# Two-layer hybrid trunk on one core: narrow products merged, padded and ordered by array tile, and constants made at the start

## Chip, cores and metric

One core of one Trainium2 chip runs the whole program. The metric is the device time of one execution in microseconds (us), the median of several runs. Engines are named as the profile names them: PE is TensorE's matmuls, PEld its weight loads, DVE VectorE, ACT ScalarE, POOL GpSimd, and SP the engine from whose queue all data transfers are issued.

## The reference

The input is 256 tokens of width 1024. Each of the two layers projects the normalized input `h` into the columns of three token mixers, runs the mixers, merges them under gates, and then runs a feed-forward part: dense in the first layer, eight experts (two per token) in the second. Cut to what the change touches:

```python
def layer(x, l):
    h = rms_norm(x) * (1 + sc_m) + sh_m
    rw_cols, ssd_cols, fox_cols, gates = split(h @ w_in[l])
    # 1. RWKV-7: token shift, low-rank decay / rate / gate, delta-rule recurrence
    r, k, v, w_lo, a_lo, g_lo = split(token_shift(rw_cols, mu))   # 512 512 512 64 64 160
    w = -softplus(-(w0 + tanh(w_lo) @ w_up)) - 0.5
    a = sigmoid(a0 + a_lo @ a_up);  g = sigmoid(g_lo) @ g_up
    if l > 0: v = v + (v_first - v) * sigmoid(v0 + (h @ v_down) @ v_up)   # v_down: 1024x32
    S_t = S_{t-1} * w_t + (S_{t-1} a_t) b_t + v_t k_t ;  y_t = S_t r_t     # per head, 64x64
    # 2. SSD: 16 heads in 4 groups, dt = softplus(dt_raw + bias), chunks of 128 tokens
    a_cum = cumsum(dt * A);  decay_ij = exp(a_cum_i - a_cum_j)             # per head, 128x128
    # 3. FoX: 8 heads of 64, softmax attention with a cumulative log-forget bias
    s = q @ k.T / 8 + F_q - F_k,  F = cumsum(log_sigmoid(f_logit + bias))
    x = x + g_m * (merged @ w_out[l]);  x = x + g_f * ffn(...)
```

## The kernel before

Activations stand with features on the 128 partitions and the 256 tokens along the free axis. Every weight arrives in float32 and is split into a high part (ACT, L156) and a low part (DVE, L157); a product of such pairs is three one-pass matmuls (`mm3`). The small matrices inside the mixers are plain float32, and the trace shows each of their products as two passes, that is two MATMUL records. Transposes (`transpose`, L131) are one pass.

A planner that simulates the engines writes each engine's order when the program is built; on the chip each engine then runs its queue in that order. `ORDER` names the steps of a layer: `r0`, `r1` are the two halves of RWKV (two 128-feature blocks each), `s0` to `s3` the SSD groups, `f0`, `f1` the halves of FoX, `G`, `m0` to `m2` gates and merges. Steps of different mixers alternate, so that the projections of one run between the dependent steps of another.

The projections use two PSUM buffers named `pd` (`dbank`), taken in turn; the mixers use four named `pm` (`mbank`) and two named `ps` (`sbank`). Places that the change touches:

- `small_cols` projects 24 columns (16 `dt`, 8 forget logits), copies them and transposes them into `dtr` (L452, L454, L456). `rwkv` then projects 288 columns from 1536 (L470), as a block of 256 and one of 32 (the last 32 of the gate LoRA), and in the second layer 32 more (`rw_v_down`, L479).
- `rwkv_half`, first stage: 16 products of 64 rows each per half (L611), head by head, copied out by DVE (L612). Second stage: a triangular inverse in six levels; each level ends in DVE transposes (L654). Its end is L682 to L691. Third stage: the recurrence over two chunks (L693 to L731). Fourth: `gu0` and `gu1` (L751, L752), the latter with 32 rows.
- `ssd` makes the cumulative sums of 16 heads (L781 to L784), high and low part; `ssd_group` copies one head's row to all partitions by two products with 16 rows (L838).
- `fox_half` transposes 64 features of q and k per head (L927, L928), and makes the bias row for partition 64 by three products with one column (L929 to L931).
- Masks and identities are built in the first layer after the first normalization (L1320 to L1372); six products (L1365) and their DVE work build `ztmask`.

## Time and profile before

| | |
|---|---|
| median of 3 runs | 2226.83 us (2225.98 to 2227.79) |
| profiled execution | 2224.52 us, of which span 2222.8 us |
| PE busy (share of the span) | 2115.0 us (95%) |
| DVE busy | 1798.8 us (81%) |
| ACT busy | 1386.1 us (62%) |
| POOL busy | 152.1 us (7%) |
| data moved | 546.68 MB, mean 246 GB/s |

The first layer's mixers stand at about 45 to 450 us, its output projection and feed-forward part at 450 to 705, the second layer's mixers at 705 to 1150, and the experts from there to the end. A PE record's duration holds the latency of the array; how fast a run of n matmuls streams is read from the starts of successive rows, or from a merged row as (length of the run minus one duration) over n-1.

### The profile page before, as it was taken

Reading aid. Unit: us, or ns where it says so; the run is one execution under the profiler, and the core shown is the slowest. Engines: PE = TensorE matmul, PEld = TensorE weight load, DVE = VectorE, ACT = ScalarE, POOL = GpSimd, SP = SyncE. Lnnn points to the kernel's source line nnn. Section 1 sums busy time; section 2 is a strip of 40 time slices with the busy share of each in tenths; the row PEclk is TensorE's granted clock in tenths of the full one; section 3 lists DMA queues with packets and bytes.
Section 4 is the critical chain, followed back from the end, with each engine's and each line's share of the span. In section 5 each row is a group of like instructions: output and inputs, shape, how many; then the busy total and the mean of one; then the engine's idle time right before and its main releaser. Section 6 shows DMA issues by size and latency. Waiting matters only on the chain.

```text
span 2222.8 us, 35724 instructions
## 1 busy us (share of the span) xinstructions
PE 2115.0 (95%) x13489; PEld 1811.2 (81%) x13489; DVE 1798.8 (81%) x2822; ACT 1386.1 (62%) x2204; POOL 152.1 (7%) x180
## 2 busy tenths in 40 slices
PE   7899899999998889989998999999999999999998
PEld 4777789998997877868998788888888887888776
DVE  4977776777776797756768999999999989999887
ACT  3454455555454545434555877878878777878775
POOL 2211200000000031211002000000000000000000
PEclk9999999999999998988998999999999999999999
DMA  8423254667884533414556999999999999999994
GB/s 304 128 83 95 77 172 156 213 198 259 294 286 137 145 108 93 138 53 130 184 176 251 337 362 359 324 368 367 374 337 352 355 362 336 342 364 368 336 363 151
DMA packets 316101, 546.68 MB, mean 246 GB/s; under 512 B 11952, under 2 KB 143536, under 8 KB 315920
## 3 DMA queue, kind: packets, MB, share of 16 engines
q1 hardware_dynamic: 315920, 544.31, 71.1%
q8 instruction: 108, 1.77, 0.3%
q14 instruction: 73, 0.60, 0.1%
HBM read 543.22 MB, written 1.05 MB: 245 GB/s over the span
## 4 chain that ended last, share of the span: by engine, by line
PE 79%; DVE 13%; issue 3%; ACT 2%; DMA 2%; POOL 0%; SPq 0%; DVEq 0%; ACTq 0%; POOLq 0%
PE pd L122 37%; PE pm L122 33%; PE ps L122 7%; DVE lo L157 5%; PE pm L131 1%; DVE u L654 1%; DMA araw<-in_ada_w_dram 1%; PE ps L131 1%; ACT hi L156 1%; DMA b<-in_ada_w_dram 1%; DVE cu L802 1%; DVE xr L1257 1%; DVE u L225 0%; DMA raw<-in_moe_w_gu_dram 0%; DVE b L612 0%
## 5 line engine op out<-in xcount | busy, mean ns | idle before, releaser
L156 ACT ACTIVATE hi<-raw 128x1024 fp32r<-128x1024 f32 (+2 forms) x1201 | 1027.7, 870 | 522.4 <-PE pd L122 277.0
L157 DVE TENSOR_TENSOR lo<-raw,hi 128x1024 fp32r<-128x1024 f32 (+2 forms) x1197 | 1154.6, 990 | 211.6 <-ACT hi L156 189.8
L122 PE MATMUL pd<-hh,hi 128*128 128x256 f32 (+2 forms) x1208 | 352.7, 293 | 15.3 <-ACT hh L362 3.9
L122 PE MATMUL pd<-hh,lo 128*128 128x256 f32 (+2 forms) x1208 | 346.5, 287 | 0.0
L122 PE MATMUL pd<-hl,hi 128*128 128x256 f32 (+2 forms) x1208 | 345.7, 286 | 0.3
L122 PE MATMUL pm<-lo,hh 128*128 128x512 f32 x672 | 266.7, 397 | 3.0 <-DVE lo L157 2.8
L122 PE MATMUL pm<-hi,hh 128*128 128x512 f32 x672 | 266.9, 397 | 0.1
L122 PE MATMUL pm<-hi,hl 128*128 128x512 f32 x672 | 263.0, 392 | 0.0
L122 PEld LDWEIGHTS pd<-hh,hi 128*128 128x128 f32 (+2 forms) x1208 | 231.9, 192 | 28.3 <-issue 5.6
L122 PEld LDWEIGHTS pd<-hh,lo 128*128 128x128 f32 (+2 forms) x1208 | 231.5, 192 | 6.1 <-issue 3.9
L122 PEld LDWEIGHTS pd<-hl,hi 128*128 128x128 f32 (+2 forms) x1208 | 232.7, 193 | 4.3 <-issue 2.3
L122 PE MATMUL pd<-lo,hi 128*128 128x512 f32 x448 | 174.7, 390 | 0.0
L122 PE MATMUL pd<-hi,hi 128*128 128x512 f32 x448 | 170.9, 391 | 0.1
L122 PE MATMUL pd<-hi,lo 128*128 128x512 f32 x448 | 167.8, 389 | 0.0
L122 PEld LDWEIGHTS pm<-lo,hh 128*128 128x128 f32 x672 | 126.8, 189 | 32.1 <-DVE lo L157 5.5
L122 PEld LDWEIGHTS pm<-hi,hh 128*128 128x128 f32 x672 | 126.5, 188 | 29.3 <-ACT hi L156 1.4
L122 PEld LDWEIGHTS pm<-hi,hl 128*128 128x128 f32 x672 | 126.7, 189 | 26.5
L122 PE MATMUL pm<-hi,more 128*128 128x512 f32 x448 | 142.1, 392 | 0.0
L122 PEld LDWEIGHTS pd<-hi,hi 128*128 128x128 f32 x448 | 84.1, 188 | 18.4 <-ACT hi L405 0.5
L122 PEld LDWEIGHTS pd<-hi,lo 128*128 128x128 f32 x448 | 84.1, 188 | 17.8
L122 PEld LDWEIGHTS pd<-lo,hi 128*128 128x128 f32 x448 | 84.1, 188 | 17.6
L122 PEld LDWEIGHTS pm<-hi,more 128*128 128x128 f32 x448 | 84.1, 188 | 17.5 <-ACT hi L156 0.3
(423 smaller groups left out, 3467.0 us busy)
## 6 DMA issues: line engine op xcount, KB each, us to landing
raw<-in_moe_w_gu_dram SPq DMA_DIRECT2D x224, 1024.0 KB, 7.0
raw<-in_moe_w_down_dram SPq DMA_DIRECT2D x110, 1024.0 KB, 6.8
raw<-in_w_in_dram SPq DMA_DIRECT2D x66, 1024.0 KB, 5.4
araw<-in_ada_w_dram SPq DMA_DIRECT2D x68, 512.0 KB, 4.3
raw<-in_ffn_w_gu_dram SPq DMA_DIRECT2D x22, 1024.0 KB, 6.8
raw<-in_ffn_w_down_dram SPq DMA_DIRECT2D x11, 1024.0 KB, 6.5
raw<-in_w_in_dram SPq DMA_DIRECT2D x16, 512.0 KB, 5.1
raw<-in_proj_ssd_dram SPq DMA_DIRECT2D x8, 1024.0 KB, 5.2
```

The lines of the kernel that those rows point to most:

```text
L122: pe.matmul(o, lhsT, rhs, start=start, stop=stop)
L131: pe.transpose(o, i, ident[:n, :n])
L156: act.activation(hi, raw, AF.Copy)
L157: minus.tensor_sub(lo, raw, hi.bitcast(F32))
L654: dve.transpose(blk(bds[ch], q)[:, odd, bcol(q)], by4(blk(pz, q))[:, odd, :])
L802: dve.scalar_tensor_tensor(cu[:, s:T], ps[:, 0:T - s], pph[:, w:w + 1], cu[:, s:T], op0=ALU.mult, op1=ALU.add)
L1257: dve.tensor_add(xr[:, t, hs], xr[:, t, hs], po)
```

## The change

`small_cols` now makes one projection of 88 columns: the 32 of the gate LoRA, 32 of `rw_v_down` (zeros in the first layer), 16 `dt`, 8 forget logits. It leaves them in `gl[:, 1, :]`, whose other partitions are zero, and transposes that tile whole. The products with `gu1` and `vup` take all 128 rows, with zeros in the padding. `cum` holds the high part on partitions 0 to 15 and the low part on 32 to 47, so that one product with 128 rows does for two with 16. In FoX the cumulative sums are made once per layer and written as a 65th feature beside k (ones beside q), and the transposes carry it. Products in the first and third stage of RWKV and at the end of the second are regrouped by the rows and columns of the array that they use. The constants (`identb`, `uincl`, `ustr`, `mmask`, `nmq`, `headsel`, `bones`, `rmask`, `icomp`, `ztmask`), by the same lines as before, move from behind the first normalization to the place between the first loads and the first products.

```diff
@@ setup
-    identr = const("identr", [16, 16], F32R)
-    act.activation(identr, ident[:16, :16], AF.Copy)
+    identr = const("identr", [P, 16], F32R)
+    dve.tensor_tensor(identr, ident[:, 0:16], ident[:, 32:48], op=ALU.add)
@@ load_lora
-        gu1 = keep("gu1", [32, RW])
-        nc.sync.dma_start(gu1, lora_g[l])
+        gu1 = keep("gu1", [P, RW])
+        pool.memset(gu1, 0.0)
+        nc.sync.dma_start(gu1[0:32], lora_g[l])
@@ accumulate
-        step = min(kin, stage[2] // w)
+        step = min(kin, 1 << (stage[2] // w).bit_length() - 1)
@@ small_cols
-        raw = load_raw(dtw[l].rearrange("p (k w) -> p k w", k=KD), KD, 24)
+        gl = mx("gl", [P, 2, T], bufs=1 + (l > 0))
+        pool.memset(gl[:, 1, :], 0.0)
+        raw = load_raw(narrow[l].rearrange("p (k w) -> p k w", k=KD), KD, 88)
         ps = dbank()
-        accumulate(ps[:24, :T], raw, (hh, hl))
-        dc = mx("t1", [24, T], bufs=2)
-        act.activation(dc, ps[:24, :T], AF.Copy)
+        accumulate(ps[:88, :T], raw, (hh, hl))
+        act.activation(gl[64:88, 1, :], ps[64:88, :T], AF.Copy)
+        if l > 0:
+            act.activation(gl[32:64, 1, :], ps[32:64, :T], AF.Copy)
+        shift(prm, gl[:32, 1, :], ps[:32, :T], 14)
+        ps = dbank().rearrange("p (a t) -> p a t", t=P)
         for t in range(2):
-            transpose(ps[:, T + t * 24:T + t * 24 + 24], dc[:, t * P:(t + 1) * P], 24)
+            transpose(ps[:, t, :], gl[:, 1, t * P:(t + 1) * P])
@@ rwkv
-        project_cols(w_in[l], 1536, 288, lambda i, ps: shift(wa if i == 0 else gl[:ps.shape[0], i - 1, :], ps, 12 + i))
+        project_cols(w_in[l], 1536, 256, lambda i, ps: shift(prm, wa if i == 0 else gl[:, 0, :], ps, 12 + i))
...
-            accumulate(ps[:32, :T], load_raw(rw_v_down.rearrange("p (k w) -> p k w", k=KD), KD, 32), (hh, hl))
-            vd = mx("wa", [32, T], bufs=2)
-            act.activation(vd, ps[:32, :T], AF.Copy)
-            vup = mx("gl", [32, RW], bufs=2)
-            nc.sync.dma_start(vup, rw_v_up)
+            vup = mx("gl", [P, RW], bufs=2)
+            pool.memset(vup, 0.0)
+            nc.sync.dma_start(vup[32:64], rw_v_up)
@@ rwkv_half, first stage
+                pss = [mbank(), mbank()]
+                for jj in J:
+                    for hb in range(2):
+                        hp = hblock(hb)
+                        mm(pss[hb][:, jj * 256:jj * 256 + 256], src[hp, jj, cs], ar[jj][hp, ch, :, :])
                 for hb in range(2):
-                    ps = mbank()
-                    hp = hblock(hb)
-                    for jj in J:
-                        mm(ps[:, jj * 256:jj * 256 + 256], src[hp, jj, cs], ar[jj][hp, ch, :, :])
                     dve.copy_predicated(dst.rearrange("p (j b) m t -> p j b (m t)", b=2)[:, :, hb],
                                         mmask.rearrange("p m t -> p (m t)").unsqueeze(1).broadcast_to([P, 2, 2 * P]),
-                                        ps.rearrange("p (q m) -> p q m", q=2))
+                                        pss[hb].rearrange("p (q m) -> p q m", q=2))
@@ rwkv_half, end of the second stage
+        yas = []
         for ch in range(2):
             py = mbank()[:, :256].rearrange("p (q t) -> p q t", q=4)
...
-            ya = unit(mx, 4, 64)
-            act.activation(ya[h1], py[h1], AF.Copy)
+            yas.append(unit(mx, 4, 64))
+            act.activation(yas[ch][h1], py[h1], AF.Copy)
+        for ch in range(2):
+            ya = yas[ch]
@@ rwkv_half, third stage
             for q, (jj, hp, f) in enumerate(heads):
-                o = pb[q % 2][:, jj, :]
-                mm(o, mk[:, q, 0, :], vrow[:, ch, f], True, ch == 0)
-                if ch == 1:
-                    mm(o, ar[jj][hp, 1, 0, :], s0[hp, jj, :], False, True)
+                mm(pb[q % 2][:, jj, :], mk[:, q, 0, :], vrow[:, ch, f], jj == 0, ch == 0 and jj == 1)
+            if ch == 1:
+                for q, (jj, hp, f) in enumerate(heads):
+                    mm(pb[q % 2][:, jj, :], ar[jj][hp, 1, 0, :], s0[hp, jj, :], False, jj == 1)
...
+            py = mbank()[:, :256].rearrange("p (j t) -> p j t", j=2)
+            for q, (jj, hp, f) in enumerate(heads):
+                mm(py[hp, jj, :], vrow[:, ch, f], mk[:, q, 1, :], jj == 0, False)
+            if ch == 1:
+                for q, (jj, hp, f) in enumerate(heads):
+                    mm(py[hp, jj, :], s0[hp, jj, :], ar[jj][hp, 1, 1, :], False, False)
...
             if ch == 0:
                 pst = mbank().rearrange("p (q f) -> p q f", f=64)
...
                 dve.tensor_tensor(s0, pst[:, 0:2, :], dec0.unsqueeze(2).broadcast_to([P, 2, 64]), op=ALU.mult)
+            for q, (jj, hp, f) in enumerate(heads):
+                mm(py[hp, jj, :], sa[:, q, :], mb[:, q, 1, :], False, jj == 1)
+            yc = unit(mx, 2, P)
+            act.activation(yc, py, AF.Copy)
@@ rwkv_half, fourth stage
-            mm(pg[:, jj * T:(jj + 1) * T], gu1[:, js], gl[0:32, 1, :], False, True)
+            mm(pg[:, jj * T:(jj + 1) * T], gu1[:, js], gl[:, 1, :], False, True)
@@ ssd and ssd_group
-            mm(ps[:16, ch * P:(ch + 1) * P], dta[:, ch * 16:ch * 16 + 16], uincl)
+            mm(ps[:48, ch * P:(ch + 1) * P], dta[:, ch * 16:ch * 16 + 48], uincl)
+        cum = mx("cum", [P, T], F32R)
+        pool.memset(cum.bitcast(F32), 0.0)
...
-                for i in range(2):
-                    mm(pc[:, e * T:(e + 1) * T], identr[:, h:h + 1].broadcast_to([16, P]), cum[:, i, :], i == 0, i == 1)
+                mm(pc[:, e * T:(e + 1) * T], identr[:, h:h + 1].broadcast_to([P, P]), cum)
@@ fox and fox_half
+        ps = mbank()
+        mm(ps[:, 0:8], uincl, nlf[:, 0:8])
+        mm(ps[:, 8:16], uincl, nlf[:, 8:16], True, False)
+        mm(ps[:, 8:16], ones, nlf[:, 0:8], False, True)
+        sums = small(16, "f", 10).rearrange("p (t h) -> p t h", t=2)
+        act.activation(sums, ps[:, 0:16].rearrange("p (t h) -> p t h", t=2), AF.Copy)
...
-            o = unit(mx, 2, 256)
+            o = mx("u", [P, 2, 4, 65 if g < 2 else 64], bufs=NUNIT)
...
+            if g == 0:
+                pool.memset(o[:, :, :, 64:65], 1.0)
+            elif g == 1:
+                pool.tensor_copy(o[:, :, :, 64], sums[:, :, 4 * hf:4 * hf + 4])
...
-                    transpose(ps[0:64, t * P:(t + 1) * P], qkv[1][:, t, f])
-                    transpose(ps[0:64, T + t * P:T + (t + 1) * P], qkv[0][:, t, f])
-                mm(ps[64:65, 0:P], nlf[:, h:h + 1], uincl)
-                mm(ps[64:65, P:2 * P], nlf[:, 8 + h:9 + h], uincl, True, False)
-                mm(ps[64:65, P:2 * P], nlf[:, h:h + 1], ones, False, True)
+                    transpose(ps[0:65, t * P:(t + 1) * P], qkv[1][:, t, h, :])
+                    transpose(ps[0:65, T + t * P:T + (t + 1) * P], qkv[0][:, t, h, :])
@@ main
     first_load(6)
     first_load(7)
+
+    identb = const("identb", [P, P], BF16)
+    dve.tensor_copy(identb, ident)
...
+        ztmask.append(ztm)
+        prev = same
+
     first_half(0)
...
-            done = norm_cols(mod_affine(l, 1, 0, prm["pp"][:, NMIX:NMIX + 8]), normed)
+            norm_cols(mod_affine(l, 1, 0, prm["pp"][:, NMIX:NMIX + 8]), normed)
             dump(f"hh{l}", hh)
-            if l == 0:
-                with tc.issue_after(done.ins):
-
-                    identb = const("identb", [P, P], BF16)
...
-            dtr = small_cols(l, mx)
+            dtr, gl = small_cols(l, mx, prm)
```

## Rows read from the trace of the kernel before

**Rows 1.** The page: the chain that ended last, by engine, as shares of the span.

```profile
PE 79%; DVE 13%; issue 3%; ACT 2%; DMA 2%; POOL 0%; SPq 0%; DVEq 0%; ACTq 0%; POOLq 0%
```

**Rows 2.** Busy time by stage: stretch, its length, then busy us (and instructions) of PE, PEld, DVE, ACT, POOL, the granted share of PE's clock, the DMA share and GB/s.

```profile
45.00:300.00 255.00, 229.83 (x1963) 195.45 (x1962) 197.00 (x480) 121.37 (x287) 52.30 (x59) 0.94 0.35 104
...
705.00:1050.00 345.00, 308.86 (x2502) 262.60 (x2503) 250.96 (x571) 167.95 (x394) 62.19 (x66) 0.91 0.38 114
1050.00:1150.00 100.00, 100.00 (x843) 94.08 (x841) 68.18 (x128) 55.79 (x120) 3.95 (x3) 1.00 0.53 168
```

**Rows 3.** The chain that ended last, by line, in the stretches 60 to 300 us (first row), 300 to 450 (second) and 735 to 1050 (third).

```profile
by line: PE pd L122 34.1%; PE pm L122 18.0%; PE ps L122 8.7%; DVE lo L157 5.7%; DVE u L654 5.3%; PE pm L131 3.4%; issue 3.2%; DVE cu L802 2.7%; ACT s L843 1.9%; ACT hi L156 1.9%; DVE b L612 1.2%; DVE u L225 0.8%; DVE s L848 0.8%; PE ps L131
by line: PE pd L122 71.2%; PE pm L122 14.3%; PE ps L122 8.9%; PE pm L131 4.2%; ACT hi L156 0.8%; PE ps L131 0.4%; ACT u L953 0.3%; issue 0.1%; ACTq L156 0.0%
by line: PE pd L122 41.5%; PE pm L122 19.0%; PE ps L122 8.4%; DVE u L654 4.5%; issue 3.7%; PE pm L131 3.7%; DVE lo L157 2.6%; DVE u L225 2.1%; DVE cu L802 1.9%; DVE b L612 1.4%; DVE u L223 1.2%; ACT hi L156 0.8%; DVE s L822 0.5%; DVE xb L80
```

**Rows 4.** PE's waits, 45 to 450 us (first row) and 705 to 1150 us (second): what waited for what, us in total, times, longest us.

```profile
PE pm L122 <- DVE u L654: 8.4, 9, 1.7
PE pm L122 <- DVE u L654: 8.5, 9, 2.4
```

**Rows 5.** PE in order of time around 305 us, in FoX: start us, length of the run us, instruction, count.

```profile
304.91 0.60 PE L131 MATMUL pm<-ident,u 128*64 128x128 f32 x4
305.44 0.60 PE L122 MATMUL pm<-uincl,sm 128*1 128x128 f32 x4
...
306.19 0.52 PE L131 MATMUL pm<-ident,u 128*64 128x128 f32 x3
```

**Rows 6.** The same around 319 us, in an SSD group.

```profile
319.14 0.28 PE L122 MATMUL pd<-hl,hi 128*128 128x256 f32 x1
319.25 0.39 PE L122 MATMUL pd<-hh,lo 128*128 128x256 f32 x2
319.57 0.73 PE L122 MATMUL ps<-cum,identr 16*128 16x256 f32 x4
320.23 0.39 PE L122 MATMUL pd<-hh,hi 128*128 128x256 f32 x1
```

**Rows 7.** The same around 85 us (a 256-column float32 product with all rows), around 265 us (fourth stage of RWKV) and 734 us (`vup`).

```profile
85.35 0.59 PE L122 MATMUL pm<-u,bones 128*128 128x256 f32 x2
85.78 0.27 PE L131 MATMUL pm<-ident,vfirst 128*128 128x128 f32 x1
...
265.83 0.70 PE L122 MATMUL pm<-gl,up 128*128 128x256 f32 x2
...
268.34 0.44 PE L131 MATMUL pm<-ident,u 128*128 128x128 f32 x2
...
734.38 0.69 PE L122 MATMUL pm<-wa,gl 32*128 32x256 f32 x2
735.00 0.39 PE L122 MATMUL pd<-hh,lo 128*128 128x256 f32 x1
```

**Rows 8.** The same around 165 and 176 us, in the third stage of RWKV.

```profile
165.41 0.44 PE L122 MATMUL pm<-s,u 64*128 64x64 f32 x4
...
166.87 0.43 PE L122 MATMUL pm<-s,u 64*128 64x64 f32 x2
...
176.36 0.44 PE L122 MATMUL pm<-u,s 64*64 64x128 f32 x4
```

**Rows 9.** The products of L611, around 90 and 780 us.

```profile
90.09 2.10 PE L122 MATMUL pm<-u,u 64*128 64x256 f32 x16
...
780.33 1.13 PE L122 MATMUL pm<-u,u 64*128 64x256 f32 x4
781.39 0.39 PE L122 MATMUL pd<-hl,hi 128*128 128x256 f32 x1
```

**Rows 10.** Mask work at 40 to 62 us, grouped by line: count, busy us, mean ns.

```profile
L1365 PE MATMUL pm<-u 32*128 32x128 f32 (+4 forms) x10 | 2.1, 308 | 0.0
L1366 DVE COPY u<-pm 128x128 f32<-128x128 f32 x6 | 1.7, 286 | 0.4 <-PE pm L1365 0.4
L1370 DVE TENSOR_TENSOR ztm<-u,ustr 128x128 bf16<-128x128 f32 x6 | 1.7, 285 | 0.0
```

**Rows 11.** The projections of 32 columns on PE at 0 to 1160 us, one of their three parts (the other two have as many): count, busy us, mean ns, idle before.

```profile
L122 PE MATMUL pd<-hh,hi 128*32 128x256 f32 x24 | 6.7, 280 | 1.0 <-ACT dtr L456 1.0
```

**Rows 12.** PE and DVE in order of time at the start of the second layer's mixers.

```profile
713.75 0.41 PE L122 MATMUL pd<-hh,lo 128*24 128x256 f32 x1
713.96 0.41 PE L122 MATMUL pd<-hh,hi 128*24 128x256 f32 x1
...
719.31 0.48 DVE L363 SCALAR_TENSOR_TENSOR hl<-h,mod,hh 128x256 fp32r<-128x256 f32 x1
...
720.86 0.28 PE L122 MATMUL pd<-hh,lo 128*128 128x256 f32 x1
...
722.53 0.30 PE L122 MATMUL pd<-hh,hi 128*32 128x256 f32 x1 [0.67 <-ACT dtr L456]
...
730.88 0.28 PE L122 MATMUL pd<-hh,hi 128*128 128x256 f32 x1
```

**Rows 13.** SP's queue and POOL in order of time in the first 20 us.

```profile
15.50 0.63 SPq L286 DMA_DIRECT2D gu<-in_lora_g_dram  x1
...
17.53 3.55 POOL L605 MEMSET b<- 128x2048 f32 x2 [14.06 <-PE ps L122]
```

More of the change, by code (lines that the diff above doesn't have):

```diff
@@ L65, in trunk @@
     ctx: ExitStack, tc: tile.TileContext,
-    x, cols, heads, dtw, ada_w, w_in, lora_up, lora_g, rw_v_down, rw_v_up, proj_rw, proj_ssd, proj_fox, w_out,
+    x, cols, heads, narrow, ada_w, w_in, lora_up, lora_g, rw_v_up, proj_rw, proj_ssd, proj_fox, w_out,
     ffn_w_gu, ffn_w_down, moe_router, moe_w_gu, moe_w_down, out, dbg=None, stop=None,
@@ L1297, in trunk @@
     first_load(7)
+    identb = const("identb", [P, P], BF16)
+    dve.tensor_copy(identb, ident)
+    uincl = const("uincl", [P, P])
+    pool.affine_select(out=uincl, in_=ones, compare_op=ALU.is_ge, fill=0.0, base=0,
+                       pattern=[[1, P]], channel_multiplier=-1)
+    ustr = const("ustr", [P, P])
+    pool.affine_select(out=ustr, in_=ones, compare_op=ALU.is_gt, fill=0.0, base=0,
+                       pattern=[[1, P]], channel_multiplier=-1)
+    mmask = const("mmask", [P, 2, P], U8)
+    dve.tensor_copy(mmask[:, 0, :], ustr)
+    dve.tensor_copy(mmask[:, 1, :], uincl)
+    nmq = const("nmq", [P, P], BF16)
+    dve.tensor_scalar(nmq, ustr, -1e30, None, op0=ALU.mult)
+    headsel = const("headsel", [P, 2])
+    pool.memset(headsel, 0.0)
+    pool.memset(headsel[0:64, 0:1], 1.0)
+    pool.memset(headsel[64:128, 1:2], 1.0)
+    bones = const("bones", [P, P])
+    pool.memset(bones, 0.0)
+    pool.memset(bones[0:64, 0:64], 1.0)
+    pool.memset(bones[64:128, 64:128], 1.0)
+    rmask = const("rmask", [P, 4, P], BF16)
+    pool.memset(rmask, 1.0)
+    pool.memset(rmask[:, :, 0:1], 0.0)
+    icomp = const("icomp", [P, P])
+    for n in range(4):
+        ns = slice(n * 32, n * 32 + 32)
+        dve.tensor_copy(icomp[ns].rearrange("p (q c) -> p q c", q=4), ident[ns, ns].unsqueeze(1).broadcast_to([32, 4, 32]))
+    ztmask = []
+    prev = ident
+    for lv in range(6):
+        m2 = 2 << lv
+        nb = P // m2
+        same = unit(mx, 1, P)[:, 0, :]
+        ind = unit(mx, 1, P)[:, 0, :]
+        pool.affine_select(out=ind[:nb], in_=ones[:nb], compare_op=ALU.is_ge, fill=0.0, base=0,
+                           pattern=[[1, P]], channel_multiplier=-m2)
+        pool.affine_select(out=ind[:nb], in_=ind[:nb], compare_op=ALU.is_ge, fill=0.0, base=m2 - 1,
+                           pattern=[[-1, P]], channel_multiplier=m2)
+        ps = mbank()
+        pe.matmul(ps[:, :P], ind[:nb], ind[:nb], start=True, stop=True)
+        dve.tensor_copy(same, ps[:, :P])
+        ztm = const(f"ztm{lv}", [P, P], BF16)
+        diff = unit(mx, 1, P)[:, 0, :]
+        dve.tensor_sub(diff, same, prev)
+        dve.tensor_mul(ztm, diff, ustr)
+        ztmask.append(ztm)
+        prev = same
     first_half(0)
```

138 lines of the change are left out of this document (38 added, 100 removed).

## The prediction

> **What bounds the kernel.** I read the chain that ended last first: PE holds 79% of it and DVE 13% [rows 1]. Then the stages. The change leaves the feed-forward parts alone; it acts in the two layers' mixers. There the reader is to separate two kinds of stretch. In the second part of each layer's mixers (FoX, the last SSD group, the merges) PE is the chain: the second row of rows 3 adds up to 99%, and in the second layer PE is busy for all of the 100 us [rows 2, 3]. In the first part PE's lines add up to about 65% of the chain in the first layer and 73% in the second; the rest is mostly DVE steps of the RWKV recurrence [rows 3], and PE is busy in 230 of 255 and 309 of 345 us [rows 2]. So a microsecond of PE work taken out is worth a full one in the second part, and in the first part about what PE's share of the chain says, 0.69 on average. That share is my exchange rate; the true one lies between 0 and 1.
>
> The price of PE's work is read from starts of successive rows, not from durations. A one-pass 256-column product costs 0.11 us [rows 6]. A change between array shapes costs extra: the product before the run of 16-row products keeps 0.20 instead of 0.11 us for its last pass (0.32 from 319.25 to 319.57 for two), and the run of four takes 0.66 where four of the usual kind would take 0.45 [rows 6].
>
> **The change, part by part.**
>
> FoX. From the first transpose to the next head's first, 304.91 to 306.19, a head takes 1.28 us; six of its ten passes are the one-column sums. Four transposes at 0.11 (the four passes at 305.44 hold 0.43) leave 0.44, so 0.84 goes per head [rows 5]. That the 65th column makes a transpose dearer no row shows; its pass still streams 128 columns of the identity, so I take nothing. 16 heads in two layers: 13.4 us. Added are six passes a layer before the halves, at 0.11: 1.3. Net 12.1, in the second part, at full rate. POOL's writes of the 65th feature are ready long before the transposes.
>
> Cumulative sums of SSD. Each pair of heads spends 0.66 plus 0.09 of the shape change; two full-height passes cost 0.23 [rows 6]. 0.52 times 16 pairs is 8.3 us. A quarter (the last group of each layer) lies in the second part at full rate, 2.1; 6.2 lie in the first part.
>
> Padding. The fourth stage's eight passes take 2.51 us, 265.83 to 268.34; at 0.215 a pass (two in 0.43, 85.35 to 85.78) they would take 1.72 [rows 7]: 0.78 in four halves, 3.1 us. `vup` takes 0.62 instead of 0.43, plus 0.09 on entry [rows 7]: 0.28 four times, 1.1 us.
>
> Recurrence. In the second chunk full-height and half-height products alternate: five runs that start 0.37 apart, 1.8 us in all [rows 8]. Grouped, I estimate 1.25 (four full passes at 0.11, eight half-height passes at the pace of the first run of rows 8, and two changes of shape). 0.55 four times is 2.2; two changes fewer in `py` and two fewer at the second stage's end give 1.2 and 0.7 at 0.09 each over all halves and chunks. Sum 4.1 us. The `s0` products of `py` work with both row halves in one PSUM bank; in the trace four such passes run in 0.44 us [rows 8], less than one after the other. The Trainium skill (TensorEngine Tiling (Array Packing), Gotcha 1) says that different row tiles cannot use one bank at a time; the trace does not bear that out here, and by the rule some 0.6 us of this term would be lost.
>
> These first-part terms (6.2, 3.1, 1.1, 4.1) make 14.5 us of PE time; at 0.69, 10.0.
>
> The products of L611. Where the planner already lets two row halves run side by side, 16 passes take about 1.8 us; where it does not, four take 1.06 [rows 9]. The new order makes pairs everywhere: four lone sets in each half, two groups of two each saving 0.3, some 2.4 us a half and 9.6 in all at most. But these sets wait for DVE's copies (L612 is itself in the chain [rows 3]), and two buffers are now taken at once. Between 0 and 9.6 I take 2.0, nearest the end at which DVE decides.
>
> Constants. Ten passes of L1365, 2.1 us, stand between the first projections, and about 0.4 of shape changes with them; at the start PE waits for loads, so they cost nothing there. DVE's part is 1.7 (L1366), 1.7 (L1370) and about as much for the rest [rows 10], 6.8 us in all, moved to where DVE waits for the first loads. Of it only the entries after about 57 us, where DVE becomes the chain, count: 1.2. Sum 3.7; ends 2.5 and 9.3. If the cover at the start were gone, the six products would delay the first normalization by at most their own 2.1 us.
>
> Narrow projections. 72 one-pass products go (24 rows of each of three parts [rows 11]); at 0.115 that is 8.3 us, 2.75 in the first layer and 5.5 in the second. It doesn't come in full. Before, PE fills the time in which the normalization delivers its eight column blocks with two groups, the 24-column one and the first 128 of the 256; in the second layer that ends at 720.86, while the last block is delivered at about 719.8 [rows 12]. After, the narrow product takes one `pd` buffer and the transposes take the other, so the 256-wide block has to wait until the narrow one has been copied out: two or three copies of ACT and one DVE step, some 1.5 us. Second layer: last block 719.8, copies to 721.4, 48 products at 0.114 to 726.9, where before the six groups end at 730.88 [rows 12]. That is 4.0 at the full clock, and -0.7 if all 48 run at the 0.21 us spacing of 713.75 to 713.96 [rows 12]; I take 2.4, a third of them slow. First layer, by the same reckoning with one group less to save, 1.1. Sum 3.5, ends -2.7 and 8.2.
>
> Waits that are added. `gu1` and `vup` are now cleared by POOL before SP may issue their loads, and behind those in SP's queue stand the first projection weights. The load of `gu1` is issued at 15.50; POOL's next work, clears that wait for PE, starts at 17.53 [rows 13]. If the planner puts the new clear ahead of those it costs nothing, which I take; behind them it could hold SP for several microseconds, the upper end of the range.
>
> **Sum.** 12.1 + 2.1 + 10.0 + 2.0 + 3.7 + 3.5 = 33.4 us. Against the profiled execution, 2224.52 us (span 2222.8, with 1.7 around it, 2.3 below the median of the runs), 2191.1; against the median, 2226.8 - 33.4 = 2193.4. The experts start earlier by as much, and their stage is not touched.
>
> **Rivals.**
>
> Waits take PE's place: in the first part every PE saving turns into waiting for DVE. For it: DVE is busy in 197 of 255 us there [rows 2]. Against it: PE's named waits are short, 8.4 us for the longest group in the first layer [rows 4]. Then 10.0 and 2.0 go: 2205.4. With the narrow term at its lower end and SP held as well, it is 2219, inside the bound of no change with a little more.
>
> The clock stays low at the mixers' start. Products are 0.21 us apart at 713 and 0.11 at 720 [rows 12], the 1.2 and the 2.4 GHz level; PE was full between. With only one narrow group, PE pauses between blocks. Then the narrow term is -2.7: 2199.6. The Trainium skill (TensorE: Matmul & The Clock Gate, HAM oscillation) says the clock is throttled by default and released by sustained activity, which speaks against thinning this stretch; the spacing agrees.
>
> The regrouping does not reach the chip, since the planner sorts by its own forecast (it already interleaves row halves that the source has in series [rows 9]): recurrence and L611 give nothing, 2.8 + 2.0: 2198.2.
>
> Better: exchange rate 1, L611, constants and narrow products at their upper ends: 12.1 + 2.1 + 14.5 + 9.6 + 9.3 + 8.2 = 55.8, 2171.
>
> Slower: the work removed was what filled the waits of the triangular inverse. 40 of its steps end in DVE's transposes (five levels, two chunks, four halves), and only 18 of them now make PE wait, 16.9 us in all, 0.42 per step [rows 4]. If every step waited the longest of the first layer, 1.7, it would be 68 us, 51 more, and the time 2244. It decides from (16.9 + 33.4)/40 = 1.26 us a step. Against it: the projections, the main filler, stay.
>
> **Chances.** Forecast 0.46; waits 0.16; low clock 0.10; no regrouping 0.12; better 0.06; slower 0.05; the stacked case near no change 0.05. The range, 2174 to 2212, leaves out most of "better", all of "slower" and the stacked case. About 0.2% (4.5 us) is what a measurement of this kernel can tell from no change: faster 0.89, same 0.06, slower 0.05.
>
> **What would show it.** Right: no one-column sums in FoX and 0.44 us per head; two passes per pair of SSD heads with no stretched pass before them; eight even passes in RWKV's fourth stage; no L1365 after 10 us; the first layer's mixers shorter by about 18 us and the second's by about 15.5. Wrong: PE's waits for L654, L612 or L648 growing by more than 10 us; products at 0.21 spacing well after the normalization ends; SP idle before 20 us; DVE's share of the chain in the first part rising by as much as PE's falls.

## The result, and the profile after

The changed kernel takes 2199.12 us (median of 4 runs, 2196.64 to 2200.93) where the kernel before takes 2227.31 on the same chip: a ratio of 0.9871, 95% interval 0.9854 to 0.9888, or 29 us less (25 to 33). A second set of five rounds gave 0.9875 (0.9852 to 0.9899). The forecast was 2193.4 with a range from 2174 to 2212, faster. The profiled execution took 2199.16 us, span 2197.1.

The first two fences answer to [rows 1] and [rows 2]. First the page's chain by engine, then busy time by stage (columns as in [rows 2]).

```profile
PE 78%; DVE 14%; issue 3%; DMA 3%; ACT 3%; POOL 0%; SPq 0%; DVEq 0%; ACTq 0%; POOLq 0%
```

```profile
45.00:300.00 255.00, 230.89 (x1921) 196.82 (x1922) 192.25 (x454) 120.97 (x288) 50.73 (x59) 0.89 0.35 102
705.00:1050.00 345.00, 310.15 (x2608) 274.00 (x2609) 261.52 (x597) 178.10 (x415) 59.19 (x66) 0.92 0.39 116
1050.00:1150.00 100.00, 98.58 (x826) 94.99 (x826) 70.79 (x129) 56.20 (x115) 2.33 (x1) 1.00 0.55 177
```

PE still holds the chain. (The granted clock is a share of 2.4 GHz; 0.50 is the level of 1.2.) In the first layer PE is as busy over the 255 us as before, though it has less to do: its granted clock in that stretch is 0.89, before 0.94. (In the second profile of the changed kernel, further down, it is 0.93.)

Most operations came out as forecast. Each group of the next fence is PE in order of time: FoX's transposes, a pair of SSD heads, the fourth stage of RWKV, the recurrence, the first stage's products, and the last products of the masks (start us, length of the run us, instruction, count; the first five answer to [rows 5 to 9]).

```profile
308.26 1.03 PE L132 MATMUL pm<-ident,u 128*65 128x128 f32 x8
309.13 0.27 PE L132 MATMUL ps<-ident,xb 128*128 128x128 f32 x1
...
321.25 0.28 PE L123 MATMUL pd<-hl,hi 128*128 128x256 f32 x1
321.37 0.40 PE L123 MATMUL ps<-cum,identr 128*128 128x256 f32 x2
321.61 0.28 PE L123 MATMUL pd<-hh,lo 128*128 128x256 f32 x1
...
299.95 0.60 PE L123 MATMUL pm<-gl,up 128*128 128x256 f32 x2
...
301.68 0.27 PE L132 MATMUL pm<-ident,u 128*128 128x128 f32 x1
...
292.11 0.66 PE L123 MATMUL pm<-s,u 64*128 64x64 f32 x8
292.70 0.66 PE L123 MATMUL pm<-b,u 128*64 128x128 f32 x8
293.29 0.65 PE L123 MATMUL pm<-u,s 64*64 64x128 f32 x8
293.87 0.39 PE L123 MATMUL pd<-hh,hi 128*128 128x256 f32 x1
...
218.07 1.13 PE L123 MATMUL pm<-u,u 64*128 64x256 f32 x8
...
222.79 1.13 PE L123 MATMUL pm<-u,u 64*128 64x256 f32 x4
...
19.33 0.79 PE L1357 MATMUL pm<-u 2*128 2x128 f32 x2 [1.82 <-POOL u L1354]
```

Eight transposes with the 65th column take 0.87 us, so a head takes 0.44, and the column costs nothing. A pair of SSD heads takes 0.24 (321.37 to 321.61) where it took 0.66, and no pass ahead of it is stretched. The fourth stage's eight passes take 1.73 us where [rows 7] have 2.51. The recurrence's eight passes with `s` stand in one run, 0.59 us to the next row, instead of three ([rows 8]). The eight `s0` products of `py` (293.29 to 293.87) take 0.58 us, as long as the eight full-height passes ahead of them, so the 0.6 us that the prediction set against them were not lost. Two things did not come. L611's regrouping (L615 after) hardly reached the chip: 13 lone sets of four passes remain, as many as before, and a lone set (222.79) is as long as eight passes whose row halves run side by side (218.07). And the masks' products, which were to be over by 10 us, wait for POOL; the last pair runs at 19.33.

What did not come as forecast are the stages. I read each stage from the starts of the same seven steps in every trace. In the changed kernel they are: the first `s + 1` of RWKV's first half, the scaling of the second half's first chunk, the first addition of the output projection, the end of the feed-forward part (the second of the two steps of that row), the same `s + 1` and scaling in the second layer, and its last merge.

```profile
66.35 0.43 DVE L520 TENSOR_SCALAR u<-u 128x512 f32<-128x512 f32 x1 [0.37 <-ACT u L519]
295.56 0.42 DVE L752 TENSOR_TENSOR u<-u,sm 128x256 f32<-128x256 f32 x1 [1.12 <-POOL sm L135]
479.69 0.41 DVE L1022 TENSOR_TENSOR xr<-xr,h 128x256 f32<-128x256 f32 x1
698.22 1.29 DVE L1069 TENSOR_TENSOR xr<-xr,otmp 128x512 f32<-128x512 f32 x2
742.78 0.42 DVE L520 TENSOR_SCALAR u<-u 128x512 f32<-128x512 f32 x1
985.00 0.42 DVE L752 TENSOR_TENSOR u<-u,sm 128x256 f32<-128x256 f32 x1 [1.19 <-POOL sm L135]
1147.68 0.41 DVE L1011 TENSOR_TENSOR b<-b,gt 128x256 f32<-128x256 f32 x1
```

The differences of these starts, for the profiled execution of each kernel in this study (us; "start", "first part" and "second part" of each layer's mixers, and between the layers the output projection with the feed-forward part):

| kernel | start 1 | first 1 | second 1 | between | start 2 | first 2 | second 2 | span |
|---|---|---|---|---|---|---|---|---|
| before | 61.2 | 227.0 | 196.6 | 220.3 | 45.8 | 246.8 | 173.3 | 2222.8 |
| before, second profile | 62.5 | 228.1 | 196.6 | 221.1 | 45.3 | 246.3 | 173.5 | 2225.1 |
| changed | 66.4 | 229.2 | 184.1 | 219.1 | 44.0 | 242.2 | 162.7 | 2197.1 |
| changed, second profile | 67.6 | 223.4 | 183.9 | 221.8 | 44.3 | 242.8 | 162.0 | 2196.1 |
| sums alone | 63.7 | 230.7 | 194.8 | 223.2 | 45.6 | 249.1 | 173.2 | 2230.8 |
| sums and FoX | 64.4 | 224.8 | 186.5 | 222.8 | 46.1 | 252.1 | 167.7 | 2213.9 |
| padding of `gu1` alone | 63.3 | 230.6 | 193.7 | 220.2 | 45.7 | 249.8 | 172.7 | 2228.2 |
| regrouping alone | 62.1 | 228.8 | 194.8 | 220.2 | 45.9 | 239.7 | 167.2 | 2212.6 |
| regrouping undone | 66.3 | 234.2 | 187.3 | 220.1 | 44.7 | 253.0 | 166.3 | 2226.5 |
| narrow products undone | 64.3 | 224.0 | 185.1 | 220.2 | 45.7 | 243.0 | 163.7 | 2200.5 |
| constants undone | 67.7 | 221.8 | 184.4 | 221.4 | 43.8 | 242.4 | 161.9 | 2197.9 |
| narrow product later | 60.6 | 222.3 | 184.3 | 220.4 | 43.9 | 238.5 | 161.3 | 2183.7 |
| narrow product in `ps` | 59.9 | 222.7 | 185.6 | 221.7 | 37.7 | 248.0 | 159.9 | 2189.7 |
| both of these | 64.5 | 223.6 | 184.0 | 225.3 | 39.7 | 246.1 | 162.4 | 2198.4 |

In the profiled pair the second parts give 12.5 and 10.6 us, 23 of the 26 that the span fell by. The first layer's start loses 5.2; the first parts give -2.2 and 4.6. So the gain sits in the second parts, and hardly at all in the first ones. These second parts are not quite the stretches where the prediction counted PE's work at full rate: they begin at 295.6 and 985.0 and hold the last steps of the recurrence, and in the second layer the regrouping alone takes 6.2 of the 10.6 us there.

A row of the table is one execution. Those of the sums alone and of the padding alone are the slowest of their kernels' runs, 3.5 and 4.4 us above the median; that of the narrow product in `ps` is 5.7 above it.

The start of the first layer shows its loss in the trace. The next fence has ACT and PE in order of time; the last row is the pause of PE that the narrow term named.

```profile
32.24 0.89 ACT L157 ACTIVATE hi<-raw 128x352 fp32r<-128x352 f32 x2 [1.65 <-DMA raw<-in_narrow_dram]
33.03 0.36 ACT L354 ACTIVATE u<-ps 128x256 f32<-128x256 f32 x1
...
46.48 0.66 PE L132 MATMUL pd<-ident,gl 128*128 128x128 f32 x2 [2.03 <-DVE gl L452]
```

ACT's queue has the split of the narrow weights ahead of the copy that the normalization waits for, and those weights land at 32.2; before, that copy ran at 28.05. (The experiments show that this is not what sets the pace.) Then the narrow product holds one `pd` buffer and its transposes the other, and PE waits for the copies. The second layer's start shows the same (PE in order of time, answers to [rows 12]):

```profile
718.26 0.66 PE L132 MATMUL pd<-ident,gl 128*128 128x128 f32 x2 [2.39 <-DVE gl L452]
718.57 0.56 PE L123 MATMUL pd<-hh,hi 128*128 128x256 f32 x1
...
722.77 0.35 PE L123 MATMUL pd<-hl,hi 128*128 128x256 f32 x1
722.96 0.29 PE L123 MATMUL pd<-hh,lo 128*128 128x256 f32 x1
723.08 0.28 PE L123 MATMUL pd<-hh,hi 128*128 128x256 f32 x1
```

The last block of the normalized input is ready at 714.6 + 0.5 us; the 256-wide block starts at 718.57 and runs at 0.21 us a product until 722.8, then at 0.11.

### The profile page after: what moved, and what is told of

Same layout as the page of the kernel before. It is cut to its first block, busy times and chain, and to the rows that moved or that the text cites. A ratio compares the mean times of both kernels' runs of the same rounds, so it can differ in the third digit from the quotient of the medians.

```text
span 2197.1 us, 35356 instructions
## 1 busy us (share of the span) xinstructions
PE 2092.7 (95%) x13301; PEld 1804.3 (82%) x13301; DVE 1798.8 (82%) x2822; ACT 1380.2 (63%) x2204; POOL 151.7 (7%) x187
## 4 chain that ended last, share of the span: by engine, by line
PE 78%; DVE 14%; issue 3%; DMA 3%; ACT 3%; POOL 0%; SPq 0%; DVEq 0%; ACTq 0%; POOLq 0%
PE pd L123 37%; PE pm L123 31%; PE ps L123 7%; DVE lo L158 6%; PE pm L132 1%; DVE u L658 1%; ACT hi L157 1%; PE ps L132 1%; DVE cu L811 1%; DMA b<-in_ada_w_dram 1%; DMA araw<-in_ada_w_dram 1%; DMA raw<-in_narrow_dram 1%; DVE xr L1270 0%; DMA raw<-in_moe_w_gu_dram 0%; DMA raw<-in_proj_ssd_dram 0%
## 5 line engine op out<-in xcount | busy, mean ns | idle before, releaser
L123 PE MATMUL pd<-hh,hi 128*128 128x256 f32 (+1 forms) x1184 | 349.4, 295 | 9.9 <-DVE cu L811 3.3
L123 PE MATMUL pd<-hl,hi 128*128 128x256 f32 (+1 forms) x1184 | 341.7, 289 | 1.8 <-DVE hl L365 1.8
L123 PE MATMUL pd<-hh,lo 128*128 128x256 f32 (+1 forms) x1184 | 340.4, 288 | 0.2 <-DVE lo L158 0.2
L123 PEld LDWEIGHTS pd<-hh,hi 128*128 128x128 f32 (+1 forms) x1184 | 231.2, 195 | 26.3 <-issue 10.2
L123 PEld LDWEIGHTS pd<-hl,hi 128*128 128x128 f32 (+1 forms) x1184 | 231.6, 196 | 8.4 <-DVE hl L365 4.6
L123 PEld LDWEIGHTS pd<-hh,lo 128*128 128x128 f32 (+1 forms) x1184 | 230.8, 195 | 3.3 <-issue 2.4
L123 PEld LDWEIGHTS pd<-hi,lo 128*128 128x128 f32 x448 | 84.0, 188 | 17.8 <-DVE lo L408 0.2
```

The lines of the kernel that those rows point to most:

```text
L123: pe.matmul(o, lhsT, rhs, start=start, stop=stop)
```

## Experiments

Each kernel was timed against the kernel before on its chip; ratios are to that, with 95% intervals.

**Which part delays the start?** Four kernels were made from the changed one. The first has its narrow products and their padding as before (each line with its old counterpart put back: `dtw`, `rw_v_down`, `project_cols(..., 1536, 288, ...)`, `gu1` and `vup` of 32 rows).

> The changed kernel (2199.1 us) with its narrow products as before: 24 columns, then 256 and 32, then 32 of v_down, and gu1 and vup with 32 rows; everything else stays changed. In the changed kernel the tanh of the decay input comes 7.8 us later in the first layer (54 for 46 us) and, measured from the start of the layer, 7 us later in the second. Theory A, the merged narrow product starves the start of the mixers (its transposes hold the second pd buffer, PE pauses and the 256-wide block runs at 0.21 us a product): without it the tanh is back at 46 to 48, the second layer's start is 7 us shorter, and of these 15 us most shows in the time, less 2.9 for the padding that also goes: 2186 to 2194. Rival B, the late start is absorbed by waits that are there anyway: the narrow term of the prediction (3.5) and 2.9 of padding come back, 2205. Rival C, the constants at the start made it late: the tanh stays at about 54, 2203 to 2206. Theory D, apart from these: between 89 and 117 us the changed kernel runs PE at the low clock, 0.21 instead of 0.11 us a product, for some 13 us; where that stretch is at the high clock in this run, the time falls by up to 13 more.

Measured: 2203.15 us, ratio 0.9892 (0.9876 to 0.9909), some 4 us slower than the changed kernel, with intervals that overlap. The tanh comes at 49.5 us (54 in the changed kernel, 46 before) and the second layer's start takes 17.8 us to it, as before (26.7 in the changed kernel). Theory A is right on where a part of the time goes at the start (64.3 instead of 66.4 and 67.6 us, where 61.2 and 62.5 stood before), and wrong on its weight: 26.7 or 17.8 us to the tanh, `s + 1` comes 44.0 or 45.7 us into the second layer. That wait is absorbed by the next one, as rival B said. With the padding gone as well, 2205 was B's number. Theory D fails too: the first layer's first part runs at 0.94 of the clock here, and the time did not fall.

The second has the constants behind the normalization, as before:

```diff
-            norm_cols(mod_affine(l, 1, 0, prm["pp"][:, NMIX:NMIX + 8]), normed)
+            done = norm_cols(mod_affine(l, 1, 0, prm["pp"][:, NMIX:NMIX + 8]), normed)
+            if l == 0:
+                with tc.issue_after(done.ins):
+                    identb = const("identb", [P, P], BF16)
...
```

> The changed kernel with its constants made behind the first normalization, as before. Theory A (the narrow product delays the start): the tanh stays at about 54 us or moves to 56, the constants' term comes back: 2200 to 2203. Rival C (ten small products of the masks and POOL's work between the first weight loads delay the first normalization and leave PE at the low clock at 20 to 30 us): the first split of the normalized input, which starts 5.2 us late in the changed kernel (35 for 30 us), is back at 30, the tanh at 48 to 50, and the time is 2192 to 2197. Rival B (neither matters for the end): 2198 to 2200.

Measured: 2199.32 us, 0.9864 (0.9846 to 0.9883): no difference to the changed kernel. The normalization starts at 31.7 instead of 34.7, but the tanh stays late (55.3): C is right about the first 3 us and they count for nothing. The constants' term of 3.7 us is not there either.

The third projects the 256 columns first and the 88 behind them:

```diff
     def rwkv(mx, l, prm, lora):
         wa = mx("wa", [P, T])
+        gl = mx("gl", [P, 2, T], bufs=1 + (l > 0))
+        pool.memset(gl[:, 1, :], 0.0)
         project_cols(w_in[l], 1536, 256, lambda i, ps: shift(prm, wa if i == 0 else gl[:, 0, :], ps, 12 + i))
+        dtr = small_cols(l, mx, prm, gl)
```

> The changed kernel with the 256-wide projection ahead of the 88 narrow columns, and the narrow product's transposes behind both. Theory A: two groups of the 256-wide block fill the normalization, no pd buffer waits for a transpose, and the tanh of the decay input comes at 46 to 49 us instead of 54; the second layer's start is 5 to 7 us shorter: 2186 to 2193. Rival B (a late start is absorbed): 2197 to 2201. Rival C (the constants delay it): the normalization still starts at 35, the tanh comes at about 51, 2194 to 2198.

Measured: 2187.64 us, 0.9824 (0.9808 to 0.9841), 11 us faster than the changed kernel, with an interval that does not touch the changed kernel's. The tanh comes at 48.6. Theory A's number, but only some 6 us of it lie in the first layer's start (60.6 us); 4 more lie in the second layer's first part.

The fourth leaves the order and takes the narrow product and its transposes into the two `ps` buffers:

```diff
-        ps = dbank()
+        ps = sbank()
         accumulate(ps[:88, :T], raw, (hh, hl))
...
-        ps = dbank().rearrange("p (a t) -> p a t", t=P)
+        ps = sbank().rearrange("p (a t) -> p a t", t=P)
```

> The changed kernel with the narrow product and its transposes in the two ps buffers, so that both pd buffers are free for the 256-wide block. Theory A by the buffers alone: PE's pause at 44.0 to 46.5 us goes and the 256-wide block runs beside the narrow one during the normalization: tanh at 49 to 51 instead of 54, second layer 3 to 5 us shorter at its start, 2190 to 2196. If not the buffers but the order in which ACT and DVE split the weights sets the pace: tanh at 53 to 54 and 2198 to 2200. Rival B: 2197 to 2201 with the tanh early.

Measured: 2185.95 us (2179.18 to 2201.09), 0.9815 (0.9784 to 0.9845). The tanh at 48.1, the shortest starts of all kernels (59.9 and 37.7), better than expected; the second layer's first part gives 6 us of that back. ACT's copy ahead of the normalization is nearly as late as in the changed kernel (32.5 us against 33.0), and the start is 6.5 us shorter all the same. So the buffers, not the order of ACT's queue, set the pace at the start.

**What is each part worth alone?** Four kernels were made from the one before. Sums alone:

```diff
-                for i in range(2):
-                    mm(pc[:, e * T:(e + 1) * T], identr[:, h:h + 1].broadcast_to([16, P]), cum[:, i, :], i == 0, i == 1)
+                mm(pc[:, e * T:(e + 1) * T], identr[:, h:h + 1].broadcast_to([P, P]), cum)
```

> The kernel before with one part of the change alone: SSD's cumulative sums on 128 rows, one product per head where there were two. By the prediction's term, with 0.69 in the first part: 6.4 us less than before. At full rate everywhere: 8.3 less. If in the first part the PE time only turns into waiting: 2.1 less. Two passes per pair of heads in some 0.23 us, without a stretched pass ahead of them.

Measured: 0.9996 (0.9984 to 1.0007), 1 us less (4 less to 2 more). The passes are as expected, the time is not. The sums and FoX's 65th feature together:

```diff
-                mm(ps[64:65, 0:P], nlf[:, h:h + 1], uincl)
-                mm(ps[64:65, P:2 * P], nlf[:, 8 + h:9 + h], uincl, True, False)
-                mm(ps[64:65, P:2 * P], nlf[:, h:h + 1], ones, False, True)
+                    transpose(ps[0:65, t * P:(t + 1) * P], qkv[1][:, t, h, :])
```

> The kernel before with that part and the 65th feature of FoX (which by itself doesn't fit beside the old sums in the on-chip memory). The prediction's terms: 12.1 for FoX and 6.4 for the sums, 18.5 less than before, and 12.1 less than with the sums alone. If FoX's heads are not wholly bound by PE, the difference to the sums alone is 6 to 9. A head takes 0.44 us instead of 1.28 from its first transpose to the next head's.

Measured: 2215.35 us, 0.9934 (0.992 to 0.9949); 13.8 us less than the sums alone (2229.10). In the table the second parts fall by 8.3 and 5.5 us against the sums alone: FoX's work came off in full, where the prediction put it.

> The kernel before with the new order of RWKV's products alone (first stage, end of the second, recurrence). The prediction's terms: 2.8 for the recurrence and 2.0 for the first stage's pairs, 4.8 less than before. If the regrouping doesn't reach the chip or doesn't count: 0, within 3. If the pairs come everywhere: up to 12 less. In the changed kernel the recurrence's runs are grouped (eight passes in 0.59 us), while 13 lone sets of four in 1.06 us remain in the first stage, where before there were 14; so I now expect 1 to 4 less.

(The edit is that of the diff for the first, second and third stage of RWKV.) Measured: 2214.26 us, 0.9931 (0.9914 to 0.9948), 15 us less (12 to 19): three times the prediction's term, and more than my lowered expectation. Nearly all of it comes in the second layer, 6.8 us in its first part and 6.2 in its second. The edit does two things that no run separates: it groups passes by array tile, and it moves steps of the dependent chain, since the products of `py` that need no `sa` now stand ahead of `psa`, and the state `s0` is made before the last products of `py`.

```diff
-        gu1 = keep("gu1", [32, RW])
+        gu1 = keep("gu1", [P, RW])
+        pool.memset(gu1, 0.0)
...
-            mm(pg[:, jj * T:(jj + 1) * T], gu1[:, js], gl[0:32, 1, :], False, True)
+            mm(pg[:, jj * T:(jj + 1) * T], gu1[:, js], gl[:, 1, :], False, True)
```

> The kernel before with gu1 and its factor padded to 128 rows, nothing else. The prediction's term: 3.1 us of PE time, at 0.69 2.1 less than before. At full rate 3.1 less. Nothing, if the fourth stage's products stand where PE has time; up to 2 more than before, if POOL's clear holds up SP's queue at the start. Eight passes in 1.72 us where there were 2.51.

Measured: 0.998 (0.9968 to 0.9992), 4.5 us less (2 to 7). The four halves' eight passes take 11.8 us before (2.51, 2.41, 2.41 and 4.44; the last at the low clock), 8.7 with the padding alone (the last, still at the low clock, 3.41) and 7.0 in the changed kernel. So the padding alone took 3.1 us off PE, as counted. POOL's clear cost nothing.

**Second profiles, and the regrouping from the other side.**

> The changed kernel once more, for a second profile and for times beside the next three. If the long stretch of the low clock in the first layer (88 to 119 us) and the one at the start of the second (699 to 723) belong to the order of the work, they stand in this profile too, and the time is 2196 to 2202. If they are chance, at least one of them is gone or shorter by 10 us and the span is 5 to 10 shorter.

Measured: 2201.36 us (2195.51 to 2211.47), 0.9875. Both answers are right, one for each stretch. In the profiles of the changed kernel (PE alone: stretch, length, busy us and instructions, granted clock, DMA share, GB/s), the first time:

```profile
88.00:118.70 30.70, 29.30 (x92) 0.50 0.35 103
699.00:722.90 23.90, 15.42 (x58) 0.50 0.30 92
```

and the second time:

```profile
88.00:118.70 30.70, 27.95 (x194) 0.94 0.45 133
697.60:721.50 23.90, 15.35 (x59) 0.50 0.28 92
```

The queues are the same program, and PE pauses for `rk` (DVE) ahead of it in both (5.6 and 5.5 us). In the first execution PE then stays at 0.50 and gets through 92 instructions in 30.7 us; in the second it gets through 194. That is a difference between two executions, not one made by the change; in the table it is 229.2 against 223.4. The stretch at the second layer's start stands in both, 23.9 us long. With the narrow products undone and in the two repaired orders the low clock lasts 10 to 14 us there, as before (10.2): the long stretch belongs to the order.

> The kernel before once more, for a second profile. If the 17 us of low clock behind the last RWKV half of the second layer (998 to 1015 us) belong to the order of the work, they are there again, as they are with the sums alone, with FoX and the sums, and with the padding alone (17.1 us each); if they are chance, they are shorter here, and the 15.6 us of the regrouping alone have another source.

It is there again. The first row is the second profile of the kernel before, from 0.3 us behind the scaling of the second half's first chunk in the second layer, the next one the same place (0.3 us behind the same step) with the regrouping alone.

```profile
1000.30:1017.40 17.10, 14.37 (x60) 0.50 0.10 27
```

```profile
991.90:1009.00 17.10, 14.51 (x99) 0.90 0.31 93
```

In this stretch no projection is left to run beside the recurrence (its DMA share is 0.10). PE has only small products that wait for each other; it falls to 0.50 and gets through 60 instructions, where the regrouped kernel gets through 99 at 0.90 and is back at FoX's projections by 999.6. There PE has small products alone as well, from 985.9 to 999.6, and the clock falls only at 998.9, for 3.4 us. Why one order loses the clock and the other keeps it, these rows don't tell.

> The changed kernel with RWKV's products in their old order. By the run with the regrouping alone (15.6 less than before) it is 12 to 18 slower than the changed kernel, 2211 to 2217, and the low clock behind the last RWKV half of the second layer lasts 14 to 17 us again instead of 3. By the prediction's term (4.8): 2204.

Measured: 2230.27 us, 1.0004 (0.9988 to 1.002): as slow as the kernel before, 29 us slower than the changed kernel. More than either theory said. The low clock behind the last RWKV half lasts 10.3 us there (1005.4 to 1015.7), less than the 14 to 17 expected. PE's idle time in the two first parts is 29.8 and 31.7 us, against 21.4 to 27.3 in the two profiles of the changed kernel. All else that the change makes gives nothing without the regrouping, although the sums and FoX alone gave 15 us.

The first part of the second layer shows what happens to work that is taken out there. One row each for the second profile of the kernel before, the sums alone, sums and FoX, the regrouping undone, then the regrouping alone and the changed kernel (PE alone, columns as above).

```profile
753.70:1000.00 246.30, 219.99 (x1860) 0.93 0.34 101
```

```profile
757.90:1007.00 249.10, 223.27 (x1844) 0.90 0.34 100
```

```profile
744.60:996.70 252.10, 226.93 (x1849) 0.89 0.33 99
```

```profile
752.40:1005.50 253.10, 221.42 (x1874) 0.91 0.34 102
```

```profile
751.90:991.60 239.70, 212.37 (x1878) 0.94 0.35 104
```

```profile
742.80:985.00 242.20, 214.94 (x1892) 0.93 0.36 106
```

Busy time times granted clock is about what PE had to do, in us at the full clock: 205, 201, 202, 201, 200 and 200 (each within 1, as the clock has two digits). With the old order of the recurrence, 3 to 4 us less to do made the stretch 3 to 7 us longer: the clock fell from 0.93 to between 0.89 and 0.91, and PE was busy for longer. With the new order about 5 us less came with the clock unchanged, and the stretch is 4 to 7 us shorter. The first layer shows the same for the sums alone (second profile of the kernel before, then the sums alone):

```profile
62.50:290.70 228.20, 204.79 (x1765) 0.93 0.34 102
```

```profile
63.70:294.40 230.70, 209.08 (x1752) 0.89 0.34 102
```

PE's idle time does not grow in either layer (23.4 and 21.6 us in the first, 26.3 and 25.8 in the second): the sums' work did not turn into waiting, it came back as a slower clock.

This is not a matter of single profiles. The mean granted clock of every timed execution is on record: 0.9655 for the kernel before (23 runs) and on the same chip 0.9629 with the sums alone (11) and 0.9702 with the regrouping alone (6); on another chip 0.9655 before (17), 0.9637 changed (6) and 0.9569 with the regrouping undone (12). Between executions of one kernel, 0.01 of this mean goes with 9 to 17 us (the eight sets of runs whose clock spread by 0.008 or more). By that estimate the clock holds 4 to 8 of the regrouping's 15 us alone, and 6 to 12 of its 29 as the last part.

> The changed kernel with both repairs: the 256-wide projection first, the narrow one behind it, in the ps buffers. By theory A one of them already takes away the waiting of the start (2187.6 and 2186.0), so both together give about the same: 2183 to 2189. If each takes away a part of its own: 2176 to 2182. The tanh of the decay input at 46 to 49 us, and no stretch of low clock over 14 us before 120 us or at the second layer's start.

Measured: 2197.09 us (2190.25 to 2209.62), 0.9851 (0.9825 to 0.9876). The repairs don't add up; together they are no better than either alone, and hardly better than the changed kernel. The tanh comes at 52.0 us, not at 46 to 49, the copy of the transposed narrow columns at 56 (48 and 52 in the single repairs), and the second layer's first part is as slow as with `ps` alone. The mean granted clock goes with the times: 0.9718 with `ps`, 0.9706 with the later product, 0.9655 with both. The fastest kernels timed are the single repairs, 2186 and 2188 us; between these two the intervals leave no order.

## Why the prediction held, and where it did not

The sum was 33.4 us and 29 were measured. That is in part luck: three terms (sums, constants, narrow projections) forecast 13.6 us together and gave some 1, the recurrence gave three times its term or more, and only FoX came out as worked out.

- **FoX** (12.1): right in place, mechanism and size; 13.8 measured.
- **Padding** (2.1 for `gu1`): the count of PE's work was right, 3.1 us of 11.8. The time is 4.5 us less (2 to 7), which fits the full rate better than the 0.69. `vup` was not run alone.
- **Sums** (6.4, from 8.3 us of PE time): the passes vanished as counted, and the time is 1 us less. The step that failed is the exchange rate, "in the first part about what PE's share of the chain says, 0.69 on average". PE's share of the chain is not a rate at which its work turns into time. SSD's products are what PE does between the dependent steps of RWKV. In the first part the sums alone gave nothing in either layer, while the work they removed came back as a lower granted clock.
- **Recurrence and L611** (2.8 + 2.0): mis-sized. 15 us alone, 29 as the last part added. L611's pairs are as few as before, the lower end of that term, which leaves the recurrence and the end of the second stage; no run takes these apart. Two reasons are in the rows: these products are the dependent chain itself, and in the second layer a part of them ran uncovered and at 0.50 of the clock, where the same work takes about twice as long (the fourth stage's passes 4.44 us instead of 2.41). Neither [rows 8] nor the counts of passes tell that; a row of windows over 998 to 1015 us would have.
- **Constants** (3.7): not there. Putting them back costs nothing measurable, although the normalization then starts 3 us earlier; the tanh is late with both. "Of it only the entries after about 57 us, where DVE becomes the chain, count" had DVE as the limit there; in the changed kernel the narrow product and its two buffers were.
- **Narrow projections** (3.5): the mechanism was right in every step, copies of ACT and DVE ahead of the transposes and the 256-wide block behind them at 0.21 us a product. Undoing it together with the padding costs some 4 us, and the padding of `gu1` by its own run is worth 4.5: about zero by itself, within these intervals. In the second layer its start is some 1.5 us shorter (2.4 forecast); in the first it is 5 us longer instead of 1.1 shorter, and undoing the narrow products takes back 2 to 3 of these. The step that was mis-sized is the wait for the two `pd` buffers, "some 1.5 us": PE waits 2.0 and 2.4 us for the copies and then runs the 256-wide block at half the clock. Without that wait (the product in `ps`) the start is shorter than before, although the split of the narrow weights (352 KB where there were 96) stands ahead of the normalization's copy there as well.

Of the rivals, "waits take PE's place" had the size right for the first parts: the two together give 2 us in the first pair of profiles and 8 in the second, not the 10 and 2 of the sum. Its mechanism is not what the rows show: with the sums alone PE's idle time did not grow, its clock fell. It also missed that the second parts would give more. "The clock stays low at the mixers' start" happened: at the second layer's start PE is at 0.50 over 24 us in both profiles, 0.21 us a product until 722.8, which is 7.7 us behind the normalization: one of the signs of being wrong that the prediction named. The next wait absorbed the loss in the second layer. The Trainium skill (TensorE: Matmul & The Clock Gate, HAM oscillation) tells of a PE that waits between bursts and starts each burst at the low clock; the trace agrees here (PE is busy in 15.42 of the 23.90 us at 0.50), and not in the 30.7 us stretch of the first layer, where PE is busy in 29.30 us and stays at 0.50 all the same. "The regrouping doesn't reach the chip" was nearly true of L611 and false of the recurrence. The times of these two, 2199.6 and 2198.2, both lie on the measured one; a time alone does not tell rivals apart. The triangular inverse did not become the bound: PE's waits for its transposes are 3.8 and 10.1 us, 8.4 and 8.5 before ([rows 4]):

```profile
PE pm L123 <- DVE u L658: 3.8, 4, 1.3
...
PE pm L123 <- DVE u L658: 10.1, 11, 1.7
```

By layer, 18 and 15.5 us were forecast. Measured from the table, the mixers of the first give 5 us in the first pair of profiles and 12 in the second pair, those of the second 17 and 16.

What stays open: why the regrouping is worth 15 us alone and 29 as the last part. Of the 30 us between the spans of the changed kernel's second profile and of the kernel with the regrouping undone, 21 lie in the two first parts (10.8 and 10.2). The planner writes a new order for each of these programs, so part of that may be the order and not the chain; no run here separates the two. Nor does a run tell the grouping by array tile from the earlier place of `py` and `s0` in the chain. That thinner work is what lowers the clock is argued from kernels in which both go together; no run changed the one and held the other.

## What to carry to other kernels

Sort the work to be removed by what it is to the path, not by its engine: here work that filled the waits of another chain was worth about nothing alone (1 us for 8.3 us of PE time), and work on the chain several times its count. Look at the granted clock of each stage before pricing anything by durations from another stage; a stretch at half the clock doubles what is removed there, and thinner work of PE in a waiting stretch went with a lower clock here, which paid the saving back. When products are merged, check who holds the buffers that the next block needs; here the merge was worth about nothing, and the same product in other buffers, or placed later, 11 to 13 us (both together only 4 to 5).

## What the runs showed that I had not expected

- The same program, executed twice, had PE at 0.50 over 30.7 us of one stretch in one execution and at 0.94 in the other, behind the same pause of 5.5 us.
- Repairs of one place don't add up: 11 and 13 us each, 4 to 5 together.
- The mean granted clock of an execution differs from kernel to kernel by more than it does between most runs of one (0.9569 with the regrouping undone, 0.9702 with the regrouping alone), and the times follow it.
